# First mixture's gathers as float32r products for two quads of experts at once, and conditioning sums stored by chunk

## The chip, the cores and the metric

One core of a Trainium2 chip runs the kernel. The metric is the device time of one execution in microseconds (us). Its five engines run side by side: TensorE (PE; its loads of the stationary operand are listed apart as PEld), VectorE (DVE), ScalarE (ACT), GpSimd (POOL) and SyncE (SP), which here issues the loads of weights. 16 DMA engines move the data.

## The reference

Two transformer blocks for 256 tokens of width 1024, one after the other, in float32. Each has a conditioning vector, a token mixer (attention and a state-space branch in the first, two kinds of attention in the second) and a mixture of 32 experts. What the change touches, cut down:

```python
# conditioning, both blocks: one row times a 1024 x 6144 matrix
mod = silu(c) @ ada_w + ada_b            # six vectors of 1024: sh1, sc1, g1, sh2, sc2, g2

# mixture of the first block: each token goes to 2 of 32 experts of width 256
h   = rms_norm(x, norm2_g) * (1 + sc2) + sh2
xs  = h[tokens of expert e]              # gather
y_e = (silu(xs @ w_gate[e]) * (xs @ w_up[e])) @ w_down[e]
x   = x + g2 * sum over experts of weight * y_e, put back at the tokens
```

## The kernel before, in words

**Weights.** All large weights stream through a ring of buffers of 2 MB (128 partitions x 4096 floats). `Ring` keeps a list of pieces in the order of their use, and SyncE issues a piece's loads (line 132) as soon as a buffer is free; a buffer is free when `ring.done()` has let go of the oldest piece in use and the engines have finished reading it. During the first mixture the ring has five lasting buffers, `NR1 = 3` more in the pool `ringq` (these take no piece from "ka", the second block's first, on), and one in `ringt` that serves until the first context piece. `ringt` takes the place of the pool `pr`, in which the routing's small tiles lie, so it can be filled when the routing is done with them.

**First mixture.** The experts are worked on in 8 quads of four, with 32 places for each expert, so a quad has 128 rows. Where an expert has more than 32 tokens, the quad is run again for the rest (`extras`, in a branch taken when the register `nv` is positive; in this data for quads 0 and 7). The order of a quad q is:

- `gather1(q)` selects the tokens. `Sm`, 0 or the token's factor of normalisation, is compared out of the positions `posm1`; 16 products on TensorE (two halves of tokens n, eight slices c of the width) multiply it with `xv1[:, n, c, :]`, the tokens themselves. The stationary operand is the token slice, whose 128 elements stand 8 floats apart, since the slices are `x1.rearrange("t n (p c) -> t n c p", c=8)`. VectorE and ScalarE in turn copy the product to `xT`, with scale and shift. `Sw` is the selection times the routing weight, transposed on TensorE and copied to `sT` for the way back.
- `up1(q)` multiplies by gate and up weights (four pieces; a buffer is let go of after each), `act1` forms silu(gate) * up, `turn1` transposes it, `down1` multiplies by the down weights (two pieces, freed at the quad's end) and adds the result to `acc` at the tokens by `sT`.

The gather of quad q + 1 stands between `act1(q)` and `turn1(q)`, and fills TensorE while the activation is formed. In quad 0 the routing weights (`weights1`) and the count of extra blocks (`extra_blocks1`, which writes `nx1`, from which `nv` is read) are computed behind the first products, by `first1`. In quads 2, 3 and 4 products for the context tokens (`ctx0` to `ctx2`, with pieces of their own) stand ahead of the quad. The second mixture (`gather2`, lines 2510 to 2526) gathers two items at a time from two float32r parts of the normalised tokens, `xh` and `xl`; this step stays as it is.

**Conditioning.** A half vector of 512 is computed in one of two ways. `mod_rows` multiplies on TensorE into four rows of partial sums, which ScalarE copies to `rows`, and `pick` adds these up while it turns the result into a column layout. For the others ScalarE, VectorE and GpSimd scale and add the weights' slices (`vectors_on` in the first block, `conditions` in the second), GpSimd's last addition writes `sums` or `part`, and `mod_sum` adds over the partitions. `pick` (8 groups) and `mod_sum` (16 groups) are each eight products on TensorE of a slice `[:, c, :]` of 64 columns, as the stationary operand, with one or two moving columns. The 512 elements lie in the order (p c), so a slice's elements stand 8 floats apart.

**Order.** Up to the first gather, and from the second block on, PE, ACT and DVE run in the order in which the code is written; in between, within the first mixture, a scheduler may move instructions within a block of code, and each engine then runs its own list in order.

Of the kernel before, what the change touches and what calls it, by code (L numbers as in the profile page):

```python
# [22 lines left out]
D = 1024  # L23
T = 256
NEG = -1e30
NR1 = 3
NR3 = 2
NU = 3
MOD0 = 1
# [128 lines left out]
def _body(tc, nc, a, off, es, stop, dump):  # L158
# [11 lines left out]
    def trps():  # L170
        return ps("tr", 2)
# [273 lines left out]
    def used(key):  # L445

        released.add(key)
        while ring.used < ring.loaded and ring.pieces[ring.used][0] in released:
            ring.done()

    def mod_rows(key, lhs, into=None):

        w = ring.get(key).rearrange("p (c f) -> p c f", c=8)
        pt = mmps()
        for c in range(8):
            j = c % 4
            PE.matmul(pt[32 * j:32 * j + 32, :], bcast(lhs[:, c, :], [P, 32]), w[:, c, :], start=(c < 4), stop=(c >= 4), tile_position=(0, 32 * j))
        used(key)
        rows = into[:, :512] if into is not None else pp.tile([P, 512], F32, tag="modrows", bufs=2, name="rows")
        S.copy(rows, pt)  # L460
        return rows

    def pick(pt, h, rows, sel=None):

        sel = k("ecol") if sel is None else sel
        n = sel.shape[1]
        rv = rows.rearrange("q (p c) -> q c p", c=8)
        for c in range(8):
            PE.matmul(pt[64 * h:64 * h + 64, n * c:n * c + n], rv[:, c, :], sel, start=True, stop=True, tile_position=(0, 64 * h))

# [4 lines left out]
    def mod_sum(s, h, dst, bias):  # L475

        r = slice(64 * h, 64 * h + 64)
        pt = trps()
        sv = s.rearrange("q (p c) -> q c p", c=8)
        for c in range(8):  # L480
            PE.matmul(pt[r, c:c + 1], sv[:, c, :], k("ones")[:, 0:1], start=True, stop=True, tile_position=(0, 64 * h))
        add_bias(dst[r], pt[r], bias[r])
# [631 lines left out]
    def vectors_on():  # L1114

        pending = None
        for tag, v, h in vectors:
# [17 lines left out]
            for c in range(0, 8, 2):  # L1135
                S.activation(w[:, c], w[:, c], AF.Identity, scale=cs[:, c])
                if c:
                    G.tensor_tensor(w[:, 0], w[:, 0], w[:, c], op=ALU.add)
                    V.scalar_tensor_tensor(w[:, 1], w[:, c + 1], cs[:, c + 1], w[:, 1], op0=ALU.mult, op1=ALU.add)
                else:  # L1140
                    V.tensor_scalar(w[:, 1], w[:, 1], cs[:, 1], None, op0=ALU.mult)
                if c == 6:
                    G.tensor_tensor(sums, w[:, 0], w[:, 1], op=ALU.add)
                    used(key)
                if c == 4 and pending:
                    pending()
                    pending = None
                yield
# [452 lines left out]
    def all_tokens(xn, rstd, A, sh, n, hT):  # L1601
# [3 lines left out]
        for h in range(2):  # L1605
# [3 lines left out]
            for c in range(4):  # L1609
                cc = 4 * h + c  # L1610
                V.tensor_scalar(hT[:, cc], pt[:, P * c:P * c + P], A[:, cc:cc + 1], sh[:, cc:cc + 1], op0=ALU.mult, op1=ALU.add)

    def gather1(q, slots, tag, sT=None, between=None):

        Sm = pw1.tile([P, 2, 4, 32], F32, tag="Sm", name="Sm")
        Sw = pw1.tile([P, 2, 4, 32], F32, tag="Sw", name="Sw")
        e4 = slice(4 * q, 4 * q + 4)  # L1620
        for n in range(2):
            V.tensor_tensor(Sw[:, n], bcast(posm1[:, n, e4, None], [P, 4, 32]), bcast(slots[:, None, :], [P, 4, 32]), op=ALU.is_equal)
            V.tensor_scalar(Sm[:, n], Sw[:, n], rstd2[:, n:n + 1], None, op0=ALU.mult)  # L1623
            if between is None:
                V.tensor_tensor(Sw[:, n], Sw[:, n], bcast(W1[:, n, e4, None], [P, 4, 32]), op=ALU.mult)
        xT = pw1.tile([P, 8, P], F32, tag="xT" + tag, name="xT")
        for c2 in range(2):
            pt = mmps() if tag else ps("sc", 2)
            for cc in range(4):
# [15 lines left out]
        for n in range(2):  # L1645
            PE.transpose(pt[:, P * n:P * n + P], Sw[:, n].rearrange("p e s -> p (e s)"), ident)
        if sT is None:
            sT = pw1.tile([P, 2, P], F32, tag="sT", bufs=2, name="sT")
        S.copy(sT, pt[:, :T].rearrange("p (c s) -> p c s", c=2))
        return xT, sT  # L1650

# [9 lines left out]
        return pg  # L1661

    def act1(pg, tag):
        act = pw1.tile([P, 256], F32, tag="act" + tag, name="act")
# [35 lines left out]

    def first1(xT):
        pg.append(up1(0, xT, ""))
        weights1()
        extra_blocks1()

    nxt = gather1(0, iota[:, 0:32], "", between=first1)
    ordered.close()
    expand(gc[:, 1, :, 0], g2b)
    r1.close()
# [109 lines left out]
    for q in range(8):  # L1819
# [17 lines left out]
        xT, sT = nxt  # L1837
# [4 lines left out]
        def extras():  # L1842
            with tc.If(nv > 0):  # L1843
                turn1(act1(up1(q, gather1(q, iota[:, 32:64], "x", sTx)[0], "x"), "x"), aTx)


        if q > 0:
            extras()
        act = act1(up1(q, xT, "", True) if q else pg[0], "")
        if q == 0:  # L1850
            extras()
            ring.done(4)
        if q < 7:
            nxt = gather1(q + 1, iota[:, 0:32], "")
        aT = pw1.tile([P, 2, P], F32, tag="aT", name="aT")
        turn1(act, aT)
        if q < 7:
            down1(q, aT, sT, q == 0, "")
        with tc.If(nv > 0):
# [75 lines left out]
    def conditions():  # L1935

        ready, fresh = None, 0
        for i in range(9):
# [10 lines left out]
            for c in range(0, 8, 2):  # L1949
                if i < 8:  # L1950
# [4 lines left out]
                    else:  # L1955
                        V.tensor_scalar(w[:, 1], w[:, 1], cs2[:, 1, 0:1], None, op0=ALU.mult)
                    if c == 6:
                        G.tensor_tensor(s, w[:, 0], w[:, 1], op=ALU.add)
# [893 lines left out]
```

## Time and profile before

| | |
|---|---|
| median of 3 runs | 2046.55 us (2046.46 to 2049.3) |
| profiled execution | 2040.22 us |
| its span, first to last instruction | 2038.5 us |
| PE busy | 1767.2 us, 87% |
| DVE, ACT, POOL busy | 854.2, 544.2, 258.6 us |
| granted clock of PE, mean | 0.931 |

The span is divided among stages: start and first attention block (to 466 us), first mixture (466 to 766), second attention block (to about 1060), second mixture (to the end). A share of busy time is a mean over these, so each stage is read by itself. Matmuls are pipelined, and float32 products are recorded as two matmuls each.

### The profile page before, as it was taken

What the parts mean: (1) busy time and instruction counts of PE and PEld (TensorE: products, weight loads), DVE (VectorE), ACT (ScalarE), POOL (GpSimd) and SP (SyncE); (2) the same over time, 40 slices, a digit from 0 to 9 for tenths busy, and PEclk for the clock granted to TensorE, in tenths of its full rate; (3) what the DMA queues carried; (4) which work ended last, traced back from release to release, by engine and by line L of the source; (5) the groups of instructions that cost most, each with busy time, mean ns of one, the idle gap of its engine ahead of it and who ended that gap; (6) DMA issues with size and microseconds to landing.
All of it is one profiled execution on the core that took longest, in us unless ns stands there. A gap on an engine that the chain in (4) does not pass through costs nothing. (4 is left out here: it accounts for less than half of the span.)

```text
span 2038.5 us, 25531 instructions
## 1 busy us (share of the span) xinstructions
PE 1767.2 (87%) x10043; PEld 990.5 (49%) x10043; DVE 854.2 (42%) x1832; ACT 544.2 (27%) x1184; POOL 258.6 (13%) x232
## 2 busy tenths in 40 slices
PE   5898999998898997899999689886899889999865
PEld 3766777876445536678864123332233333333211
DVE  7998878543312237886644112211121221221112
ACT  4442566332001115565532011110021111121001
POOL 2576312110000003630110000000000000000000
PEclk8898889898999998899979899998899999999986
DMA  8634235867889977743347999999999999899996
GB/s 262 232 114 161 99 124 179 276 239 271 319 319 395 393 294 214 256 172 94 151 167 326 420 420 419 425 422 422 416 422 419 421 423 419 340 420 418 424 421 252
DMA packets 172666, 630.82 MB, mean 309 GB/s; under 512 B 25424, under 2 KB 32016, under 8 KB 152048
## 3 DMA queue, kind: packets, MB, share of 16 engines
q1 hardware_dynamic: 172112, 628.04, 79.3%
q8 instruction: 89, 1.46, 0.3%
q10 hardware_dynamic: 288, 0.52, 0.1%
q0 software_dynamic: 128, 0.39, 0.1%
q14 instruction: 49, 0.40, 0.1%
HBM read 627.88 MB, written 1.05 MB: 309 GB/s over the span
## 5 line engine op out<-in xcount | busy, mean ns | idle before, releaser
L2553 PE MATMUL mm<-w,xT 128*64 128x512 f32 x1472 | 329.3, 601 | 1.3 <-DMA w<-in_w_gu 1.3
L2553 PEld LDWEIGHTS mm<-w,xT 128*64 128x64 f32 x1472 | 102.8, 138 | 204.2 <-issue 197.4
L2644 PE MATMUL o<-w,aT 128*64 128x512 f32 x640 | 150.7, 606 | 2.5 <-DMA w<-in_w_dn 2.5
L2587 PE MATMUL mm<-w,xT 128*32 128x512 f32 x768 | 104.6, 675 | 39.9 <-DMA w<-in_w_gu 39.9
L2562 DVE TENSOR_SCALAR g<-mm 128x512 f32<-128x512 f32 x23 | 15.9, 692 | 262.7 <-PE mm L2553 262.7
L2821 POOL TENSOR_TENSOR fin<-acc,fin 128x512 f32<-128x512 f32 x1 | 1.3, 1275 | 975.6 <-DVE acc L2819 975.6
L718 DVE TENSOR_TENSOR lo<-w,hi 128x512 fp32r<-128x512 f32 x126 | 102.2, 824 | 26.9 <-ACT hi L717 24.9
L705 PE MATMUL mm<-hTh,scratch 128*128 128x256 f32 x392 | 98.3, 317 | 10.0 <-DVE scratch L718 10.0
L717 ACT CAST hi<-w 128x512 fp32r<-128x512 f32 x126 | 76.7, 620 | 62.0 <-PE mm L705 54.2
L2619 PE MATMUL o<-w,aT 128*32 128x512 f32 x384 | 69.1, 752 | 25.7 <-DMA w<-in_w_dn 23.9
L2644 PEld LDWEIGHTS o<-w,aT 128*64 128x64 f32 x640 | 45.1, 139 | 87.5 <-issue 80.3
L2564 ACT ACTIVATE s<-g 128x512 f32<-128x512 f32 x23 | 14.5, 632 | 272.9 <-DVE g L2562 272.9
L705 PEld LDWEIGHTS mm<-hTh,scratch 128*128 128x128 f32 x392 | 71.7, 204 | 28.1 <-issue 14.1
L1657 PE MATMUL mm<-w,xT 128*32 128x512 f32 x640 | 74.4, 612 | 6.6 <-DVEq L1843 2.7
L2659 DVE SCALAR_TENSOR_TENSOR yl<-yy,wc,yh 128x512 fp32r<-128x512 f32 (+1 forms) x30 | 21.4, 748 | 137.4 <-ACT yh L2658 137.2
L2587 PEld LDWEIGHTS mm<-w,xT 128*32 128x32 f32 x768 | 23.0, 117 | 108.1 <-DMA w<-in_w_gu 61.9
L705 PE MATMUL mm<-hT3h,lo 128*128 128x256 f32 x192 | 60.6, 316 | 8.7 <-DVE lo L718 6.1
L2649 ACT COPY yy<-o 64x512 f32<-64x512 f32 x40 | 23.2, 580 | 157.6 <-PE o L2644 157.2
L1632 PEld LDWEIGHTS sc<-Sm,x 128*128 128x128 f32 x256 | 61.6, 334 | 6.6 <-issue 5.0
L2674 DVE TENSOR_TENSOR acc<-acc,sc 128x512 f32<-128x512 f32 x56 | 37.0, 685 | 66.4 <-PE sc L2666 66.4
L1632 PE MATMUL sc<-Sm,x 128*128 128x128 f32 x256 | 63.1, 410 | 1.3 <-DVE Sm L1623 1.2
L705 PE MATMUL mm<-scratch 128*128 128x256 f32 x216 | 63.8, 295 | 0.0
(706 smaller groups left out, 3532.0 us busy)
## 6 DMA issues: line engine op xcount, KB each, us to landing
w<-in_w_gu SPq DMA_DIRECT2D x128, 2048.0 KB, 20.3
w<-in_w_dn SPq DMA_DIRECT2D x63, 2048.0 KB, 23.2
w<-in_w_in SPq DMA_DIRECT2D x20, 2048.0 KB, 9.5
w<-in_moe_w_gate SPq DMA_DIRECT2D x32, 1024.0 KB, 10.5
w<-in_moe_w_up SPq DMA_DIRECT2D x32, 1024.0 KB, 12.5
w<-in_moe_w_down SPq DMA_DIRECT2D x32, 1024.0 KB, 13.8
w<-in_ada_w SPq DMA_DIRECT2D x12, 2048.0 KB, 9.8
w<-in_w_mod SPq DMA_DIRECT2D x12, 2048.0 KB, 8.9
```

The lines of the kernel that those rows point to most:

```text
L705: PE.matmul(out, x, y, start=start and i == 0, stop=stop and i == 2)
L717: S.copy(hi, src)
L718: return parts, lambda: V.tensor_tensor(lo, src, hi.bitcast(F32), op=ALU.subtract)
L1632: PE.matmul(pt[:, P * cc:P * cc + P], xv1[:, n, c, :], Sm[:, n].rearrange("p e s -> p (e s)"), start=(n == 0), stop=(n == 1))
L1657: PE.matmul(pg[32 * j:32 * j + 32, :].rearrange("p (j f) -> p j f", j=2), xT[:, c, 32 * j:32 * j + 32], w[:, c % 2], start=(c == 0), stop= ...
L2553: PE.matmul(pg[i][64 * j:64 * j + 64, :], bcast(ident[:, q:q + 1], [P, 64]) if c < 0 else xT[:, c, :], bgu if c < 0 else w[:, o:o + 512], ...
L2587: PE.matmul(pg[32 * t:32 * t + 32, :], xT[:, c, :], w[:, 512 * ij:512 * ij + 512], start=False, stop=(c == 7), tile_position=(0, 32 * t))
L2619: PE.matmul(pd[32 * t:32 * t + 32, :], aT[:, f % 4, 2 * (1 - e) + f // 4, :], w[:, 512 * j:512 * j + 512], start=False, stop=(f == 7), til ...
L2644: PE.matmul(pd[64 * j:64 * j + 64, :], aT[:, f % 4, f // 4, :], w[:, 512 * j:512 * j + 512], start=False, stop=(f == 7), tile_position=(0, ...
L2649: S.copy(y[:, 512 * j:512 * j + 512], pd[64 * j:64 * j + 64, :])
L2659: V.scalar_tensor_tensor(yl[:, o], y[:, o], back[1], yh[:, o].bitcast(F32), op0=ALU.mult, op1=ALU.subtract)
L2674: V.tensor_tensor(o, o, pc, op=ALU.add)
```

## The change

- **Gathers.** `normalised1`, called in `first1` behind the first products and ahead of `weights1`, splits the normalised tokens into float32r parts `xh1` and `xl1`, each slice contiguous. `gather1s` then gathers two quads at once: a selection `Sms` of 256 columns of 0 and 1, 32 float32r products, four banks of PSUM, `xTs` of two quads. `back1s` forms `Sw` and `sT` of both. It is called in quads 0, 2, 4 and 6, for (1, 2), (3, 4), (5, 6) and (7, 7). In odd quads nothing stands between `act1` and `turn1`. `gather1` stays for quad 0 and for the extra tokens.
- **Buffers.** `NR1` goes from 3 to 2, so seven lasting buffers are left. Some tiles share tags (`Sw` and both activations have "act"), and in quad 0 `turn1` comes ahead of `extras`.
- **Conditioning.** `rows`, `sums` and `part` are written in the order (c p), so that the slices that `pick` and `mod_sum` load are contiguous; ScalarE's copy and GpSimd's last addition write with a spacing of 64 floats.

```diff
-NR1 = 3
+NR1 = 2
...
+    def by_chunk(t):
+
+        return t.rearrange("q (c p) -> q p c", c=8)
...
-        S.copy(rows, pt)
+        S.copy(by_chunk(rows), pt.rearrange("q (p c) -> q p c", c=8))
...
-        rv = rows.rearrange("q (p c) -> q c p", c=8)
+        rv = rows.rearrange("q (c p) -> q c p", c=8)
...
-        sv = s.rearrange("q (p c) -> q c p", c=8)
+        sv = s.rearrange("q (c p) -> q c p", c=8)
...
-                    G.tensor_tensor(sums, w[:, 0], w[:, 1], op=ALU.add)
+                    G.tensor_tensor(by_chunk(sums), w[:, 0].rearrange("q (p c) -> q p c", c=8), w[:, 1].rearrange("q (p c) -> q p c", c=8), op=ALU.add)
...
+    xh1 = pw1.tile([P, 2, 8, P], F32R, name="xh1")
+    xl1 = pw1.tile([P, 2, 8, P], F32R, name="xl1")
+
+    def normalised1():
+        for n in range(2):
+            S.activation(xh1[:, n], xv1[:, n], AF.Identity, scale=rstd2[:, n:n + 1])
+            V.scalar_tensor_tensor(xl1[:, n], xv1[:, n], rstd2[:, n:n + 1], xh1[:, n].bitcast(F32), op0=ALU.mult, op1=ALU.subtract)
+
+    def gather1s(qs):
...
+        xT = pw1.tile([P, 8, T], F32, tag="xT", name="xTs")
+        for c0 in range(0, 8, 2):
+            pt = ps("sc", 2)
+            for c in range(2):
+                for n in range(2):
+                    for x in (xl1, xh1):
+                        PE.matmul(pt[:, T * c:T * c + T], x[:, n, c0 + c, :], Sm[:, n], start=(n == 0 and x is xl1), stop=(n == 1 and x is xh1))
+            for c in (c0, c0 + 1):
+                i = pt[:, T * (c - c0):T * (c - c0) + T]
+                if c % 2:
+                    S.activation(xT[:, c], i, AF.Identity, scale=A2[:, c:c + 1], bias=sh2[:, c])
+                else:
+                    V.tensor_scalar(xT[:, c], i, A2[:, c:c + 1], sh2[:, c], op0=ALU.mult, op1=ALU.add)
+        return xT, lambda: back1s(qs, xT, Sm)
...
         pg.append(up1(0, xT, ""))
+        normalised1()
         weights1()
...
         act = act1(up1(q, xT, "", True) if q else pg[0], "")
+        aT = pw1.tile([P, 2, P], F32, tag="aT", name="aT")
         if q == 0:
+            turn1(act, aT)
             extras()
             ring.done(4)
-        if q < 7:
-            nxt = gather1(q + 1, iota[:, 0:32], "")
-        aT = pw1.tile([P, 2, P], F32, tag="aT", name="aT")
-        turn1(act, aT)
+        if q % 2 == 0:
+            _, backs1 = gather1s((q + 1, min(q + 2, 7)))
+        if q:
+            turn1(act, aT)
+        if q % 2 == 0:
+            quads = backs1()
```

How this stands on the engines, at three places. ScalarE (ACT) in quad 0, behind the copies of the first gather, before (`ge` and `gsc` are the routing weights, `g2b` an expanded gain, `act` the activation):

```order
L1637 ACTIVATE xT<-sc,sh_132,A_134 128x128 x4
L1566 ACTIVATE ge_4087,gsc_4088<-lg,gsc_4088 128x4
L1568 ACTIVATE gsc_4088<-gsc_4088 128x1
L1566 ACTIVATE ge_4118,gsc_4119<-lg,gsc_4119 128x4
L1568 ACTIVATE gsc_4119<-gsc_4119 128x1
L1665 ACT_TABLE_LOAD
L1665 ACTIVATE act<-mm 128x256
L1649 COPY sT<-tr 128x256
L491 COPY g2b<-mm 128x4x128 x2
```

and now:

```order
L1689 ACTIVATE xT<-sc,sh_132,A_134 128x128 x4
L1623 ACTIVATE xh_4170<-x_68,rstd_3796 128x1024 x2
L1570 ACTIVATE ge_4087,gsc_4088<-lg,gsc_4088 128x4
L1572 ACTIVATE gsc_4088<-gsc_4088 128x1
L1570 ACTIVATE ge_4118,gsc_4119<-lg,gsc_4119 128x4
L1572 ACTIVATE gsc_4119<-gsc_4119 128x1
L495 COPY g2b<-mm 128x4x128 x2
L1701 COPY sT<-tr 128x256
L1717 ACT_TABLE_LOAD
L1717 ACTIVATE act<-mm 128x256
L1726 COPY aT<-tr 128x256
```

The two passes over all tokens stand ahead of the routing weights, the activation has moved behind the copies of `g2b` and `sT`, and its transposes' copy `aT` now belongs to this place.

TensorE (PE) from the end of the first products of quad 2 to its down products, before:

```order
L1657 MATMUL mm<-w_4624,xT 32x512 x8
L1632 MATMUL sc<-Sm,x_68 128x128 x16
L1646 MATMUL tr<-C,Sw 128x128 x2
L1673 MATMUL tr<-C,act 128x128 x2
```

and now, in the same place (16 of the products `sc<-Sms` stand ahead of the transposes of `act`, 16 behind):

```order
L1709 MATMUL mm<-w_4672,xTs 32x512 x8
L1640 MATMUL sc<-Sms,xl_4171 128x256
L1640 MATMUL sc<-Sms,xh_4170 128x256
...
L1725 MATMUL tr<-C,act 128x128 x2
L1640 MATMUL sc<-Sms,xl_4171 128x256
...
L1659 MATMUL tr<-C,Sw 128x128
L1736 MATMUL mm<-w_4752,aT 32x512
L1659 MATMUL tr<-C,Sw 128x128 x2
```

One block of 16 became 32 shorter products with the transposes laid between them; in quad 1 the place between first products and transposes is empty.

SyncE (SP) from quad 1's first piece on, before:

```order
L132 DMA w_4158<-in_moe_w_gate 128x4x512
L132 DMA w_4158<-in_moe_w_up 128x4x512
L132 DMA w_4161<-in_moe_w_gate 128x4x512
L132 DMA w_4161<-in_moe_w_up 128x4x512
L132 DMA w_4287<-in_moe_w_gate 128x4x512
L132 DMA w_4287<-in_moe_w_up 128x4x512
L1840 TENSOR_LOAD nx_3800
```

and now:

```order
L132 DMA w_4158<-in_moe_w_gate 128x4x512
L132 DMA w_4158<-in_moe_w_up 128x4x512
L132 DMA w_4290<-in_moe_w_gate 128x4x512
L132 DMA w_4290<-in_moe_w_up 128x4x512
L1893 TENSOR_LOAD nx_3800
```

Ahead of the branch of quad 0 two pieces of quad 1 are issued where three were.

## Rows read from the trace of the kernel before

**Rows 1.** four stretches: busy us of PE, PEld, DVE, ACT, POOL; clock, DMA share, GB/s

```profile
205.00:440.00 235.00, 220.60 (x1526) 179.00 (x1525) 162.56 (x458) 120.16 (x294) 60.11 (x47) 0.91 0.54 177
466.00:766.00 300.00, 273.44 (x1562) 153.90 (x1562) 80.83 (x200) 41.14 (x100) 1.40 (x2) 0.98 0.88 331
570.00:745.00 175.00, 159.20 (x918) 88.09 (x914) 41.46 (x98) 21.24 (x52) 1.40 (x2) 0.98 1.02 386
795.00:925.00 130.00, 116.06 (x774) 95.65 (x773) 110.34 (x230) 74.07 (x172) 57.21 (x51) 0.91 0.68 227
```

**Rows 2.** timeline of PE, first mixture: start, length in us, instructions

```profile
466.27 7.95 PE L1632 MATMUL sc<-Sm,x 128*128 128x128 f32 x32 [1.20 <-DVE Sm L1623]
474.15 7.07 PE L1657 MATMUL mm<-w,xT 128*32 128x512 f32 x64
...
483.37 7.86 PE L1632 MATMUL mm<-Sm,x 128*128 128x128 f32 x32
...
574.75 7.88 PE L1632 MATMUL sc<-Sm,x 128*128 128x128 f32 x32
...
731.22 7.07 PE L1657 MATMUL mm<-w,xT 128*32 128x512 f32 x64
...
763.77 1.12 PE L1693 MATMUL sc<-y,sT 128*128 128x512 f32 x2 [0.20 <-DVE acc L1695]
```

**Rows 3.** waits of PE from 466 to 766: total us, times, longest

```profile
PE mm L1684 <- ACT aT L1674: 6.5, 8, 0.9
```

**Rows 4.** timeline of SP: two issues of weight pieces

```profile
479.95 0.37 SPq L132 DMA_DIRECT2D w<-in_moe_w_gate  x1
...
493.36 0.38 SPq L132 DMA_DIRECT2D w<-in_moe_w_gate  x1
```

**Rows 5.** lines by shape, PEld: busy us, mean ns of one load

```profile
L1632 PEld LDWEIGHTS sc<-Sm,x 128*128 128x128 f32 x256 | 61.6, 334 | 6.6 <-issue 5.0 <-DVE Sm L1623 1.6
...
L2518 PEld LDWEIGHTS sc<-Sm,xh 128*128 128x128 f32 x112 | 21.9, 195 | 0.9 <-issue 0.8
...
L481 PEld LDWEIGHTS tr<-C,sums 128*64 128x64 f32 x128 | 16.1, 215 | 0.7
```

**Rows 6.** timeline of PE at three other places

```profile
217.29 2.08 PE L481 MATMUL tr<-C,sums 128*64 128x1 f32 x16
...
455.42 1.87 PE L1467 MATMUL mm<-rw,xr 128*128 128x36 f32 x16
...
1215.74 0.28 PE L2518 MATMUL sc<-Sm,xh 128*128 128x256 f32 x1
...
1217.41 0.28 PE L2518 MATMUL sc<-Sm,xh 128*128 128x256 f32 x1
```

**Rows 7.** lines by shape, ACT and then DVE, whole span

```profile
L2464 ACT ACTIVATE xT<-sc,sh,A 128x256 f32<-128x256 f32 x28 | 15.8, 563 | 22.1 <-DVE xT L2466 21.9
...
L2454 ACT ACTIVATE xh<-x,r 128x1024 fp32r<-128x1024 f32 x2 | 4.2, 2166 | 0.0
...
L460 ACT COPY rows<-mm 128x512 f32<-128x512 f32 x4 | 2.3, 580 | 7.1 <-PE mm L457 7.1
...
L491 ACT COPY fgb<-mm 128x512 f32<-128x512 f32 x2 | 2.2, 1080 | 8.0 <-PE mm L490 8.0
...
L2466 DVE TENSOR_SCALAR xT<-sc,A,sh 128x256 f32<-128x256 f32 x28 | 15.1, 541 | 13.5 <-PE sc L2518 13.5
...
L2455 DVE SCALAR_TENSOR_TENSOR xl<-x,r,xh 128x1024 fp32r<-128x1024 f32 x2 | 4.2, 2088 | 0.3 <-ACT xh L2454 0.3
```

**Rows 8.** timeline of DVE in the first quad

```profile
475.53 0.14 DVE L1565 TENSOR_SCALAR gsc<-t 128x1 f32<-128x1 f32 x1
...
479.64 0.16 DVE L1582 CAST nx<-qm 1x8 int32<-1x8 f32 x1
...
480.10 0.47 DVE L1643 TENSOR_TENSOR Sw<-Sw,W 128x128 f32<-128x128 f32 x2
```

**Rows 9.** waits of PE from 205 to 440 us

```profile
PE tr L1308 <- DVE e L1302: 4.2, 6, 1.5
```

More of the change, by code (lines that the diff above doesn't have):

```diff
@@ new lines, in gather1s @@
+    def gather1s(qs):
+        Sm = pw1.tile([P, 2, T], F32R, tag="Sms", name="Sms")
+        for i in range(2):
+            e4 = slice(4 * qs[i], 4 * qs[i] + 4)
+            for n in range(2):
+                V.tensor_tensor(Sm[:, n, P * i:P * i + P].rearrange("p (e s) -> p e s", e=4), bcast(posm1[:, n, e4, None], [P, 4, 32]),
+                                bcast(iota[:, None, 0:32], [P, 4, 32]), op=ALU.is_equal)
+        xT = pw1.tile([P, 8, T], F32, tag="xT", name="xTs")
+        for c0 in range(0, 8, 2):
+            pt = ps("sc", 2)
+            for c in range(2):
+                for n in range(2):
+                    for x in (xl1, xh1):
[7 more added lines that the diff above has]
+        return xT, lambda: back1s(qs, xT, Sm)
@@ new lines, in back1s @@
+    def back1s(qs, xT, Sm):
+        out = []
+        for i in range(1 if qs[0] == qs[1] else 2):
+            e4 = slice(4 * qs[i], 4 * qs[i] + 4)
+            Sw = pw1.tile([P, 2, 4, 32], F32, tag="act", name="Sw")
+            for n in range(2):
+                V.tensor_tensor(Sw[:, n], Sm[:, n, P * i:P * i + P].bitcast(F32).rearrange("p (e s) -> p e s", e=4),
+                                bcast(W1[:, n, e4, None], [P, 4, 32]), op=ALU.mult)
+            pt = trps()
+            for n in range(2):
+                PE.transpose(pt[:, P * n:P * n + P], Sw[:, n].rearrange("p e s -> p (e s)"), ident)
+            sT = pw1.tile([P, 2, P], F32, tag="sT", bufs=3, name="sT")
+            S.copy(sT, pt[:, :T].rearrange("p (c s) -> p c s", c=2))
+            out.append((xT[:, :, P * i:P * i + P], sT))
+        return out
@@ L1613, in gather1 @@
     def gather1(q, slots, tag, sT=None, between=None):
-        Sm = pw1.tile([P, 2, 4, 32], F32, tag="Sm", name="Sm")
-        Sw = pw1.tile([P, 2, 4, 32], F32, tag="Sw", name="Sw")
+        Sm = pw1.tile([P, 2, 4, 32], F32, tag="Sms", name="Sm")
+        Sw = pw1.tile([P, 2, 4, 32], F32, tag="act", name="Sw")
         e4 = slice(4 * q, 4 * q + 4)
@@ L1625, in gather1 @@
                 V.tensor_tensor(Sw[:, n], Sw[:, n], bcast(W1[:, n, e4, None], [P, 4, 32]), op=ALU.mult)
-        xT = pw1.tile([P, 8, P], F32, tag="xT" + tag, name="xT")
+        xT = pw1.tile([P, 8, T if not tag else P], F32, tag="xT" + tag, name="xT")[:, :, :P]
         for c2 in range(2):
@@ L1647, in gather1 @@
         if sT is None:
[L1648 removed]
+            sT = pw1.tile([P, 2, P], F32, tag="sT", bufs=3, name="sT")
         S.copy(sT, pt[:, :T].rearrange("p (c s) -> p c s", c=2))
@@ L1663, in act1 @@
     def act1(pg, tag):
-        act = pw1.tile([P, 256], F32, tag="act" + tag, name="act")
+        act = pw1.tile([P, 256], F32, tag="act", name="act")
         S.activation(act, pg[:, :256], AF.Silu)
@@ L1702, in first1 @@
         pg.append(up1(0, xT, ""))
+        normalised1()
         weights1()
         extra_blocks1()
-    nxt = gather1(0, iota[:, 0:32], "", between=first1)
+    quads = [gather1(0, iota[:, 0:32], "", between=first1)]
     ordered.close()
@@ L1836, in _body @@
             expand(fgc, fgb)
-        xT, sT = nxt
+        xT, sT = quads.pop(0)
         aTx = pw1.tile([P, 2, P], F32, tag="aTx", name="aTx")
@@ L1957, in conditions @@
                     if c == 6:
-                        G.tensor_tensor(s, w[:, 0], w[:, 1], op=ALU.add)
+                        G.tensor_tensor(by_chunk(s), w[:, 0].rearrange("q (p c) -> q p c", c=8), w[:, 1].rearrange("q (p c) -> q p c", c=8), op=ALU.add)
                         used(key)
```

## Prediction

> **What bounds the kernel now.** I first read the kernel by stretches [rows 1]: for each, the busy time of TensorE against the stretch, and the share of the DMA engines. Three stretches touch the change. From 205 to 440 us (first attention block, with twelve of the conditioning sums) TensorE is busy 220.6 of 235 us and the DMA share is 0.54: TensorE bounds it. From 795 to 925 us (second attention block, eight sums) TensorE has 116.1 of 130 us, VectorE 110.3, so the two are close. From 466 to 766 us, the first mixture, TensorE has 273.4 of 300 us, and the DMA share is 0.88. In its middle, 570 to 745 us, the DMA engines are full (1.02, 386 GB/s) while TensorE is still 91% busy. Next the waits: the longest in total of TensorE in the mixture is 6.5 us, for a copy of ScalarE, and no load of weights is in that list [rows 3]. So the mixture is bound by TensorE today, but the loads run at their full rate just behind it. That second limit decides what a shorter TensorE can bring.
>
> The sum is made in the profiled execution (2040.22 us, span 2038.5); the median of the runs shown is 2046.55, 6.33 us above it, and I carry the difference over unchanged. A change of 0.2%, 4.1 us, is about what this kernel's measurement can tell from none.
>
> **Gathers on TensorE.** A quad's gather is now 16 float32 products, recorded as 32 matmuls, and takes 7.95, 7.86 or 7.88 us in one piece [rows 2]. Seven of them (quads 1 to 7) go: 7 x 7.88 = 55.2 us. The quad 0 gather and the two for extra tokens (quads 0 and 7) stay. Four gathers of a pair of quads come, 32 float32r matmuls of 256 columns each. The second mixture already does this very step: 15 of its matmuls start from 1215.74 to 1217.41 us [rows 6], 0.119 us apart, so 32 take 3.8 us. A bank's two copies out of PSUM follow one another, 563 ns on ScalarE and 541 ns on VectorE [rows 7]; with two banks the third and fourth wait for them, and I take 5 us a pair, 20 us in all. (Bounds: 3.8, or 7 if the copies hold up each bank.) In quads 1, 3 and 5 no gather hides the activation between the first products and their transposes any more: about 1 us each, 3 us. TensorE alone is therefore 55 - 20 - 3 = 32 us shorter from quad 1 on.
>
> **First quad.** The split into two parts now stands, in program order, ahead of the routing weights. Its price is known from the same pair of instructions in the second mixture: 2166 ns on ScalarE and 2088 ns on VectorE for each half [rows 7], VectorE one half behind. Beginning when the copies of the first gather end, near 476 us, it is over at 476.1 + 2 x 2.17 + 2.09 = 482.6. The routing chain on VectorE, which began at 475.53, starts 7.1 us later; its count of extra blocks moves from 479.64 to 486.7 and the weighted selection, now done at 480.57, to 487.7 [rows 8]. TensorE was free for the extra gather at 483.37 [rows 2]. Now it waits for the transposes of that selection until 487.7, and behind them for the transposes of the first activation, which the change puts ahead of the extra tokens and which on ScalarE now queues behind the copy of the selection: some 4 us more of short instructions (estimate). The extra gather begins near 492.2: 9 us lost. Below nothing is excluded, since nothing hides it; above, 12, if the clock falls in the pause. TensorE's sum for the mixture is then 32 - 9 = 23 us shorter.
>
> **Loads.** One ring buffer goes, so during the first quad one piece of 2.1 MB fewer is fetched. The piece that SyncE issued at 479.95 moves with the count of extra blocks; the next, issued at 493.36 when the extra products let go of the first buffer [rows 4], moves to 502.4. From there 42.5 pieces are left (two of quad 1's gate and up weights, its two of down weights, six each for quads 2 to 7, and two and a half of context weights), 89.1 MB. At 386 GB/s that is 231 us, and I add 3 us for a gap when the ring is empty after the first quad: the last piece lands at 736, the last of gate and up weights two pieces (11 us) before it, at 725. What follows it today is the rest of the last quad, from the end of the extra products at 731.22 + 7.07 = 738.3 to 763.77 + 1.12 = 764.9 [rows 2], 26.6 us, plus 1.8 us for the last quarter of those products: 753. The same count for today's kernel, 41.5 pieces from 493.36, gives 736 against the 764.9 measured, so today the loads have 29 us in hand and afterwards nothing. TensorE's own limit is 764.9 - 23 = 742. The later one decides, 753, and since neither runs without hiccups I take 757: **8 us gained** of the 23. Bounds: 23, if loads never bind, and a loss of 18 (rival below).
>
> **Conditioning sums.** The 24 groups of `pick` and `mod_sum` each load eight slices of 64 columns, whose elements stand 32 bytes apart, and take 2.08 us for 16 records, 130 ns each [rows 6]. Spread columns load slowly here: 334 ns for 128 of them in the old gather against 195 ns for 128 contiguous ones in the second mixture's, and 215 ns for the 64 of the sums [rows 5]. A contiguous float32 operand with few moving columns is the router: 16 records in 1.87 us [rows 6], 117 ns for 128 columns, so 58 ns for 64. A group falls from 2.08 to 0.93 us: 1.15 us. Of TensorE's clock the rows show 0.91 of full in both stretches, before and behind the groups, and I leave that.
>
> How much counts? Twenty groups lie in the two stretches where TensorE is the busiest. Its waits there are short ones on VectorE (4.2 us over six for the softmax rows [rows 9]), one within 10 us or so of nearly every group. A wait swallows the gain if VectorE is itself the limit there, and passes it on if VectorE was waiting for TensorE; with VectorE at 69% of the first stretch and 85% of the second I take 0.55: 20 x 1.15 x 0.55 = 12.7. The four groups at the start wait for loads, and only the last counts: 1.15 less 0.5 for ScalarE's copy, which now writes spread elements (1080 against 580 ns [rows 7]). **13 us gained**; bounds 0 and 24. The sixteen sums of GpSimd also write spread elements, for which no row has a price; were every GpSimd instruction of the second stretch half as long again, it would be busy 86 of 130 us, and the sum is read only a vector later, so I take nothing.
>
> The Trainium skill, page "TensorE: Matmul & The Clock Gate", section "LDWEIGHTS (loading the stationary operand)", says that a load takes its number of columns divided by 1.2 in ns, and names no dependence on their spacing: 53 ns for 64. By that rule this part would gain nothing, and the sum would be 8 us; the 334 against 195 ns above speak against it.
>
> **Sum.** 8 + 13 = 21 us: 2040.22 - 21 = 2019 in the profiled execution, and 2046.55 - 21 = **2025.5 us** as the median of runs. What follows the mixtures' ends is shifted whole: the second mixture starts when its routing is known.
>
> **Rivals.** *Loads do not bind.* If seven buffers and 386 GB/s suffice, the mixture gains TensorE's 23 us, and with 13 the kernel takes 2010.5. For it: no wait on a load today [rows 3]. Against: full DMA engines in 175 of its 300 us [rows 1]. Chance 0.15.
>
> *The layout brings nothing*, because the waits behind each group swallow it or because spacing does not matter to a load of 64 columns: 8 us alone, 2038.5. For it: VectorE at 85% in the second stretch; against, the two load rows. Chance 0.15.
>
> *The missing buffer starves the queue* (slower). During the context products and the extra tokens, which use one buffer or none, TensorE frees little. If with one buffer less all pieces ahead land before the next is freed, the DMA engines idle for up to one more piece, 5.4 us, each time: some five times, 27 us, turning 8 gained into 18 lost, so 2051.5 with the sums' 13. It decides once these gaps pass 21 us together. For it: the share over the mixture, 0.88, shows such gaps already; against, most of them lie before 570 us. Chance 0.08.
>
> **Numbers.** My forecast has 0.62, its own range 2016 to 2035 (mixture from 0 to 15 us, sums from 7 to 18, not both at one end). Over all cases I give 2008 to 2042, which leaves out the slower rival and little else. Faster by over 0.2%: 0.85 (nearly all of the forecast, the first rival, most of the second); within: 0.06; slower: 0.09.
>
> **What would show it.** Right: new matmuls of the pair about 0.12 us apart; TensorE idle near 9 us between 483 and 492 us; waits of TensorE for gate, up and down weights in quads 5 and 6 (some 15 to 20 us), DMA full from about 505 to 735 us; the mixture 8 us shorter from its first gather to its last product, which then stands near 750 us as the sums shift it too; groups of the sums near 0.9 us. Wrong: no wait for a load, or groups still at 2 us, or DMA gaps of several us in every quad.

## The result, and the profile after

The changed kernel takes 2023.74 us (median of 4 runs, 2019.08 to 2027.47) against 2046.51 for the kernel before: ratio 0.9886, 95% interval 0.9862 to 0.9911, so 23 us or 1.1% faster. The prediction was 2025.5 us. The profiled execution took 2022.03 us with a span of 2020.0.

First the same stretches as in [rows 1], in the view by windows of the kernel after; the second line is the first mixture from its first gather to its last product, and the fourth a part of it. The columns are the stretch and its length, the busy us of PE, PEld, DVE, ACT and POOL, the granted clock, the DMA share and GB/s.

```profile
205.00:440.00 235.00, 216.07 (x1527) 173.36 (x1526) 171.61 (x469) 124.57 (x302) 59.69 (x48) 0.93 0.58 193
449.74:742.90 293.16, 250.70 (x1466) 119.27 (x1466) 78.30 (x175) 41.72 (x88) 1.40 (x2) 0.93 0.91 342
570.00:745.00 175.00, 146.29 (x824) 62.22 (x822) 43.02 (x88) 21.13 (x51) 1.40 (x2) 0.93 1.03 392
640.00:690.00 50.00, 36.60 (x200) 12.29 (x201) 7.60 (x17) 2.55 (x6) 0.00 (x0) 0.80 1.03 399
795.00:925.00 130.00, 113.43 (x807) 88.53 (x807) 110.71 (x248) 77.03 (x184) 45.48 (x45) 0.91 0.57 191
```

Two things are to be seen. The first gather starts at 449.74 us instead of 466.27 [rows 2]: 16.5 us are won before the mixture begins. The mixture lasts 293.16 us instead of 764.89 - 466.27 = 298.62 [rows 2]: 5.5 us are won in it. TensorE is busy 250.7 us there, so it is idle for 42.5; the DMA engines are full in its second half as before, and TensorE is no longer: 146.29 of 175 us against 159.20 [rows 1].

The timeline of TensorE in the first quad of the kernel after (start, length, and in brackets the idle time ahead with what ended it), to be read beside [rows 2, 8]:

```profile
449.74 7.95 PE L1684 MATMUL sc<-Sm,x 128*128 128x128 f32 x32 [1.20 <-DVE Sm L1675]
457.62 7.07 PE L1709 MATMUL mm<-w,xT 128*32 128x512 f32 x64
464.63 2.05 PE L494 MATMUL mm<-C,gc 128*128 128x128 f32 x16
470.54 0.66 PE L1698 MATMUL tr<-C,Sw 128*128 128x128 f32 x2 [3.86 <-DVE Sw L1695]
473.81 0.70 PE L1725 MATMUL tr<-C,act 128*128 128x128 f32 x2 [2.61 <-DVE act L1718]
475.39 7.91 PE L1684 MATMUL mm<-Sm,x 128*128 128x128 f32 x32 [0.88 <-DVE Sm L1675]
...
493.12 0.28 PE L1640 MATMUL sc<-Sms,xh 128*128 128x256 f32 x1
493.23 0.27 PE L1640 MATMUL sc<-Sms,xl 128*128 128x256 f32 x1
```

The extra gather (475.39) starts 25.65 us after the first gather; before it was 483.37 - 466.27 = 17.10 [rows 2]. The 8.6 us between are the pause that the prediction put at 9. Three waits for VectorE make up 7.35 us of it: 3.86 for the weighted selection, which comes behind the split; 2.61 for the activation, which on ScalarE now queues behind the copy of that selection; and 0.88 for the next selection. The last two lines are the new pair gather: one matmul each 0.12 us.

The waits of TensorE in the mixture of the kernel after (total us, times, longest), beside [rows 3]:

```profile
PE mm L1709 <- DMA w<-in_moe_w_up: 8.6, 3, 4.0
PE tr L1725 <- DVE act L1718: 8.3, 7, 2.6
PE tr L1698 <- DVE Sw L1695: 3.9, 1, 3.9
...
PE mm L1736 <- ACT aT L1726: 2.1, 4, 0.5
PE mm L1736 <- DMA w<-in_moe_w_down: 1.6, 2, 1.0
```

Loads stand in this list now, for 8.6 + 1.6 = 10.2 us; before there were none. They fall in quads 5 and 6, as the timeline of the same kernel shows:

```profile
639.94 5.36 PE L1709 MATMUL mm<-w,xTs 128*32 128x512 f32 x48 [1.21 <-ACTq L1896]
649.30 3.40 PE L1709 MATMUL mm<-w,xTs 128*32 128x512 f32 x16 [4.00 <-DMA w<-in_moe_w_up]
...
656.69 1.92 PE L1736 MATMUL mm<-w,aT 128*32 128x512 f32 x4 [0.98 <-DMA w<-in_moe_w_down]
...
676.18 2.98 PE L1709 MATMUL mm<-w,xTs 128*32 128x512 f32 x16 [2.21 <-DMA w<-in_moe_w_up]
681.56 3.64 PE L1709 MATMUL mm<-w,xTs 128*32 128x512 f32 x16 [2.40 <-DMA w<-in_moe_w_up]
```

In this stretch (640 to 690 us, above) the granted clock is 0.80: between its waits TensorE runs a part of the time at the lower of its two levels. The 48 products ahead of the longest wait take 5.36 us, 16 behind it 3.40.

The prediction's path ran through the last piece of gate and up weights. Its issue by SyncE, the same issue in the view of the DMA queue (KB, us to landing), and the extra products of quad 7, which use it first:

```profile
698.53 2.58 SPq L132 DMA_DIRECT2D w<-in_moe_w_up  x1
...
w<-in_moe_w_up SPq DMA_DIRECT2D x1, 1024.0 KB, 14.5
...
709.17 7.07 PE L1709 MATMUL mm<-w,xT 128*32 128x512 f32 x64
```

It lands at 713.0 us, about 1 us before the last quarter of these products needs it; the last product of the mixture ends 29.9 us later.

Last the conditioning sums: a group in the timeline of TensorE in the kernel after, beside the 2.08 us of [rows 6]:

```profile
214.94 1.09 PE L485 MATMUL tr<-C,sums 128*64 128x1 f32 x16
```

And lines by shape of the same kernel, of PEld, ACT and POOL in turn (busy us, mean ns of one), beside [rows 5, 7]:

```profile
L485 PEld LDWEIGHTS tr<-C,sums 128*64 128x64 f32 x128 | 8.3, 138 | 0.8
...
L464 ACT COPY sums<-mm 128x512 f32<-128x512 f32 x4 | 4.3, 1074 | 11.4 <-PE mm L461 11.4
...
L2015 POOL TENSOR_TENSOR part<-w 128x512 f32<-128x512 f32 x8 | 11.3, 1418 | 4.5 <-DVE w L2011 4.0
```

A load of 64 columns takes 138 ns instead of 215, a group 1.09 us instead of 2.08. ScalarE's copy pays for the spread writes as forecast (1074 against 580 ns); GpSimd's spread write costs nothing that shows (1418 ns; the kernel before has 1409 at that place).

### The profile page after: what moved, and what is told of

Read it like the earlier page. It is cut to its first block, busy times and chain, and to the rows that moved or that the text cites. A ratio compares the mean times of both kernels' runs of the same rounds, so it can differ in the third digit from the quotient of the medians.

```text
span 2020.0 us, 25309 instructions
## 1 busy us (share of the span) xinstructions
PE 1729.8 (86%) x9947; PEld 935.7 (46%) x9947; DVE 858.8 (43%) x1810; ACT 549.1 (27%) x1174; POOL 257.8 (13%) x232
## 5 line engine op out<-in xcount | busy, mean ns | idle before, releaser
L2610 PE MATMUL mm<-w,xT 128*64 128x512 f32 x1472 | 334.0, 608 | 0.0
L2644 PE MATMUL mm<-w,xT 128*32 128x512 f32 x768 | 105.2, 679 | 38.0 <-DMA w<-in_w_gu 38.0
L2878 POOL TENSOR_TENSOR fin<-acc,fin 128x512 f32<-128x512 f32 x1 | 1.3, 1272 | 980.7 <-DVE acc L2876 980.7
L1709 PE MATMUL mm<-w,xTs 128*32 128x512 f32 x448 | 56.7, 651 | 16.1 <-DMA w<-in_moe_w_up 8.6
L709 PE MATMUL mm<-hT3l,hi 128*128 128x256 f32 x192 | 56.1, 292 | 0.4 <-DVE hT3l L705 0.4
L709 PE MATMUL mm<-hT3h,hi 128*128 128x256 f32 x192 | 55.8, 291 | 0.0
## 6 DMA issues: line engine op xcount, KB each, us to landing
w<-in_moe_w_gate SPq DMA_DIRECT2D x32, 1024.0 KB, 14.1
```

Source lines behind the costliest of these rows:

```text
L709: PE.matmul(out, x, y, start=start and i == 0, stop=stop and i == 2)
L1709: PE.matmul(pg[32 * j:32 * j + 32, :].rearrange("p (j f) -> p j f", j=2), xT[:, c, 32 * j:32 * j + 32], w[:, c % 2], start=(c == 0), stop= ...
L2610: PE.matmul(pg[i][64 * j:64 * j + 64, :], bcast(ident[:, q:q + 1], [P, 64]) if c < 0 else xT[:, c, :], bgu if c < 0 else w[:, o:o + 512], ...
L2644: PE.matmul(pg[32 * t:32 * t + 32, :], xT[:, c, :], w[:, 512 * ij:512 * ij + 512], start=False, stop=(c == 7), tile_position=(0, 32 * t))
```

## The experiments

Two theories stood against each other. The prediction's: the gathers give TensorE more than 20 us, the loads take most of it back, and the sums give about 13 us. The other, from the two profiles alone: the sums give 16 to 18 us and the gathers 5. In the table the stretch of the mixture is from the start of the first gather to the end of the last product, in the profiled execution.

| kernel | median, us | ratio to before (95%) | mixture, us |
|---|---|---|---|
| after, first comparison | 2023.74 | 0.9886 (0.9862 to 0.9911) | 293.16 |
| after_again | 2020.64 | 0.9885 (0.9861 to 0.9910) | 292.09 |
| e1_gathers_alone | 2035.56 | 0.9947 (0.9931 to 0.9962) | 293.24 |
| e9_gathers_again | 2034.89 | 0.9962 (0.9946 to 0.9979) | 291.88 |
| e2_sums_alone | 2031.54 | 0.9928 (0.9913 to 0.9944) | 298.73 |
| e8_second_block | 2040.80 | 0.9977 (0.9964 to 0.9991) | 300.32 |
| e4_before_seven | 2044.86 | 0.9990 (0.9975 to 1.0005) | 301.88 |
| e3_split_early | 2020.46 | 0.9870 (0.9849 to 0.9891) | 287.35 |
| e3_again | 2017.17 | 0.9867 (0.9843 to 0.9891) | 286.82 |
| e7_long_runs | 2017.92 | 0.9879 (0.9854 to 0.9903) | 288.04 |

Two more, e5 and e6, have one run each, and their profiles alone are used.

**The gathers alone.** In the changed kernel, the sums go back to spread columns:

```diff
-        S.copy(by_chunk(rows), pt.rearrange("q (p c) -> q p c", c=8))
+        S.copy(rows, pt)
-        rv = rows.rearrange("q (c p) -> q c p", c=8)
+        rv = rows.rearrange("q (p c) -> q c p", c=8)
-        sv = s.rearrange("q (c p) -> q c p", c=8)
+        sv = s.rearrange("q (p c) -> q c p", c=8)
```

(and the two sums of GpSimd likewise).

> The changed kernel with the conditioning sums as they were (spread columns); gathers in pairs, seven ring buffers kept. By the prediction's own terms the mixture's part is 8 us: ratio to before 0.996. By the trace after, which has the mixture 5.5 us shorter (293.2 against 298.6 us from its first gather to its last product), 0.997. If instead the gathers carry nearly all of the gain and the sums little (the rival in which the layout brings nothing), 0.989 to 0.991. The sum groups should take about 2.08 us again.

> The gathers alone once more (sums with spread columns), because the first comparison gave 10.8 us (7.8 to 14.1) while the profiles put the mixture only 6 to 7 us shorter. By the profiles and by the prediction's 8 us the ratio is 0.996 to 0.997; by the first comparison 0.9947. If it comes out near 0.9947 again, some 4 us are gained outside the mixture.

Measured: 10.8 us (7.8 to 14.1) the first time and 7.8 us (4.3 to 11) the second. The prediction's 8 lies in both intervals; the mixture in the two profiles is 5.4 and 6.7 us shorter than 298.62. So the first figure stands at the upper end, and at least half of the gain is seen in the mixture; whether a few microseconds more come from elsewhere is below what these runs can tell.

**The sums alone.** The opposite edit, on the kernel before.

> The kernel before with the conditioning sums kept contiguous, gathers and eight buffers as they were. By the prediction 13 us of gain, ratio 0.9936, of which about 8 before the first mixture and 5 in the second attention block. By the trace after, 16.5 us before the first mixture and 1.6 in the second block: 0.991 to 0.992. If the layout brings nothing, 0.998 to 1.002. Groups of 1.09 us instead of 2.08.

Measured: 14.7 us (11.5 to 17.8), and the mixture is as it was (298.73). With the gathers' 8 to 11 this is the whole change: the parts add up. The 16.5 us that the two profiles show ahead of the mixture were too many, and the runs show why: from the first sum group to the first gather the six profiled kernels with spread sums in the first block took 242.4 to 249.0 us (mean 246.1), and the kernel before happened to be the longest of them. The seven with contiguous sums took 233.4 to 240.4 (mean 236.2). So 9.9 us arrive at the mixture.

TensorE's busy time in this stretch falls by more, from 227.6 to 212.0 us in the mean, and its idle time rises from 18.5 to 24.2. The twelve groups save 12 x 0.99 = 11.9 of these 15.6 us; other instructions became shorter too. Clearest are the 64 products of `mod_rows`, by lines of the kernel before and of the kernel after, from the first sum group to the first gather:

```profile
L457 PE MATMUL mm<-w,cs 128*32 128x512 f32 x64 | 10.7, 801 | 0.0
...
L461 PE MATMUL mm<-w,cs 128*32 128x512 f32 x64 | 7.7, 598 | 0.0
```

They take 739 to 802 ns in the six kernels with spread sums and 598 ns in all seven others. The first 16 stand right behind a sum group, in the timelines of before and after:

```profile
377.95 3.50 PE L457 MATMUL mm<-w,cs 128*32 128x512 f32 x16
...
368.91 1.92 PE L461 MATMUL mm<-w,cs 128*32 128x512 f32 x16
```

And by windows, over the stretch that holds all 64 and the four groups of `pick` there, before and after:

```profile
377.00:420.50 43.50, 43.50 (x311) 34.15 (x311) 14.30 (x28) 11.99 (x19) 4.96 (x4) 0.87 0.94 299
...
368.80:403.50 34.70, 34.03 (x312) 27.27 (x311) 15.51 (x29) 14.18 (x20) 5.09 (x5) 1.00 1.03 329
```

The granted clock is 1.00 instead of 0.87, though the profile shows TensorE without a pause there before (43.50 us busy of 43.50). In all runs these products go with the layout; what lowers the clock beside spread sums was not tried by itself.

**The eight sums of the second block alone.** On the kernel before:

```diff
-                        G.tensor_tensor(s, w[:, 0], w[:, 1], op=ALU.add)
+                        G.tensor_tensor(s.rearrange("q (c p) -> q p c", c=8), w[:, 0].rearrange("q (p c) -> q p c", c=8), w[:, 1].rearrange("q (p c) -> q p c", c=8), op=ALU.add)
```

with `mod_sum` reading contiguous columns for these eight only.

> The kernel before with only the eight sums of the second attention block kept contiguous. By the prediction's share of 0.55 they give 5 us: ratio 0.9975. By the profiles so far, in which the stretch from the mixture's end to the eighth group is 151 to 153.3 us with contiguous sums and 151.7 to 155.1 with spread ones, 1 to 2 us: 0.999 to 0.9995. If they give all that a group saves, 8 us, 0.996, and then the first block's twelve gave only some 6 of the 14 us that the sums alone gave.

Measured: 4.7 us (1.8 to 7.4), where the prediction's share gave 5. The profiles show less: from the mixture's end to the end of the eighth group the mean is 153.1 us over eight kernels with contiguous sums in this block, and 155.5 over five with spread ones, 2.4 us, with single runs from 152 to 157. From the mixture's end to the end of the span the means are 1276.8 and 1277.2, with single runs from 1272 to 1281. So the 2.4 us lie inside the interval of the timing, and whether more is gained behind the eighth group no profile shows.

**One buffer less, nothing else.** On the kernel before:

```diff
-NR1 = 3
+NR1 = 2
```

> The kernel before with seven ring buffers instead of eight, nothing else. By the prediction today's loads have 29 us in hand, so a buffer less costs little: ratio 1.000 to 1.002, with few or no waits of TensorE for weights. By the rival in which the missing buffer starves the queue, up to 27 us: ratio 1.005 to 1.013, with gaps of several us in the DMA engines after each freed buffer.

Measured: 0.9990 (0.9975 to 1.0005), no cost that can be told. Its mixture is 3.3 us longer than in the kernel before (301.88), but TensorE waits for no load in it; e8, with the mixture untouched, has 300.32, so part of this is scatter. The loads of the kernel before had time in hand, as the prediction counted, though perhaps not its 29 us: e8, whose mixture is that of the kernel before, has one wait of 1.7 us for a load. The rival of the starving queue falls as it was put, with today's loads; what the missing buffer costs in the changed kernel, where the loads bind, was not run. A piece fetched earlier would there be worth at most its own 5.4 us (estimate: 2.1 MB at the 392 GB/s of 570 to 745 us).

**Fewer loads.** Of each quad's two pieces of down weights only one is loaded, in the kernel before (e5) and in the changed kernel (e6):

```diff
-        for e in (4 * q, 4 * q + 2):
+        for e in (4 * q,):
             pieces.append((("dn1", e), lambda t, e=e: load_dn1(t, e)))
...
-                    w = ring.get(("dn1", 4 * q + j // 2 * 2))...
+                    w = ring.get(("dn1", 4 * q))...
...
-        ring.done(2)
+        ring.done()
```

(These kernels leave out half of the down weights; half of the experts multiply by another's.)

> The kernel before with half of the first mixture's down weights left out: the second pair of experts of each quad computes with the first pair's weights, 8 of 51 pieces of 2.1 MB fewer. In the kernel before, TensorE waits for no load in the mixture, so by the theory that TensorE alone bounds it the mixture stays at 298.6 us (within 1). If loads bound it too, it gets up to 43 us shorter (8 pieces of 5.4 us).

> The changed kernel with the same half of the down weights left out. By the prediction's step TensorE's own limit is 23 us under the kernel before, so the mixture falls from 293.2 to 275.6 us, with the first quad's stall of 8.6 us still in it, and TensorE's 10.2 us of waits for up and down weights go. If loads do not bind and the gain was lost elsewhere, it stays at 291 to 294 us. If besides the waits the lower clock behind them costs time, the products at 636 to 651 ns each fall back to the 595 to 612 ns that they took before.

The view by windows over the mixture, of e5:

```profile
464.42:762.58 298.16, 272.91 (x1562) 154.66 (x1562) 79.53 (x197) 40.12 (x98) 1.41 (x2) 0.97 0.76 281
```

And of e6:

```profile
457.15:726.76 269.61, 238.52 (x1466) 116.15 (x1466) 78.31 (x175) 41.77 (x88) 1.41 (x2) 0.96 0.86 316
```

With fewer loads the kernel before stays where it was (298.16 against 298.62), and the changed kernel falls from 293.16 to 269.61 us. So the loads do not bind the mixture before, and they take at least 23 us of it after. This is the clearest of the runs: it shows TensorE's own gain (298.2 - 269.6 = 28.6 us) and what the loads take back, apart. Both are lower bounds, since in e6 too TensorE waits 3.2 us for loads:

```profile
PE mm L1709 <- DMA w<-in_moe_w_down: 2.2, 2, 1.2
...
PE tr L1725 <- DMA w<-in_moe_w_up: 1.0, 1, 1.0
```

The view by lines of the kernel after, for the products of TensorE in the mixture (busy us, mean ns of one, idle time before them):

```profile
L1709 PE MATMUL mm<-w,xTs 128*32 128x512 f32 x448 | 56.7, 651 | 16.1 <-DMA w<-in_moe_w_up 8.6 <-DVEq L1896 2.7 <-ACTq L1896 2.6
L1736 PE MATMUL mm<-w,aT 128*32 128x512 f32 x256 | 39.1, 636 | 3.6 <-ACT aT L1726 2.1 <-DMA w<-in_moe_w_down 1.6
```

And the same of e6:

```profile
L1709 PE MATMUL mm<-w,xTs 128*32 128x512 f32 x448 | 51.9, 610 | 7.2 <-DVEq L1896 2.7 <-DMA w<-in_moe_w_down 2.2 <-ACTq L1896 1.4
L1736 PE MATMUL mm<-w,aT 128*32 128x512 f32 x256 | 32.4, 596 | 2.1 <-ACT aT L1726 2.1
```

Of the 23.6 us between the two, idle time is 42.5 - 31.1 = 11.4 and busy time 250.7 - 238.5 = 12.2, nearly all of it in these two groups (4.8 + 6.7): the same instructions take longer. The granted clock over the mixture is 0.93 in the one and 0.96 in the other. So the loads cost their waits and about as much again in slower products; that these are slower because of the clock behind the waits is read from the rows, not tried by itself, and how much of it would have been waits at the full clock stays open.

**The split earlier.** In the changed kernel, the split is issued behind the selection of the first gather and ahead of its copies, where ScalarE is idle from 442 to 454 us and VectorE from 450 to 454:

```diff
+        if ahead is not None:
+            ahead()
         xT = pw1.tile([P, 8, T if not tag else P], F32, tag="xT" + tag, name="xT")[:, :, :P]
...
     def first1(xT):
         pg.append(up1(0, xT, ""))
-        normalised1()
         weights1()
...
-    quads = [gather1(0, iota[:, 0:32], "", between=first1)]
+    quads = [gather1(0, iota[:, 0:32], "", between=first1, ahead=normalised1)]
```

> The changed kernel with the split of the tokens placed ahead of the first gather, where ScalarE and VectorE have nothing to do (12 us and 4 us idle), instead of ahead of the routing weights. The extra gather should then start about 17 us after the first gather, not 25.6. If the last load sets the end of the mixture and its issues hang on the extra products of the first quad (the prediction's step), the mixture is 8 us shorter than after's 293.2: ratio 0.984 to 0.985. If the stall is only traded for later waits on loads, the mixture stays within 2 us and the ratio at 0.988. If the loads do not bind at all, again 8 us, but without TensorE's waits for weights growing.

> The changed kernel once more, beside the next run on the same chip. By the sum of the two parts run alone (0.9947 and 0.9928), 0.9875; by the first comparison 0.9886. Sum groups 1.09 us; from the first gather to the last product 293 us.

> The changed kernel with the split ahead of the first gather, once more, beside the changed kernel itself. By its first profile its mixture is 5.8 us shorter than the changed kernel's (287.35 against 293.16), which would be 0.9971 of the changed kernel: 0.984 to 0.986 of before. If what it gains there is given back in the load-bound second mixture, within 0.001 of the changed kernel.

The timeline of VectorE in the first of the two runs of this version:

```profile
451.13 4.06 DVE L1624 SCALAR_TENSOR_TENSOR xl<-x,rstd,xh 128x1024 fp32r<-128x1024 f32 x2
455.11 0.40 DVE L1693 TENSOR_SCALAR xT<-sc,A,sh 128x128 f32<-128x128 f32 x1
```

And that of TensorE:

```profile
450.75 7.96 PE L1686 MATMUL sc<-Sm,x 128*128 128x128 f32 x32 [1.20 <-DVE Sm L1675]
...
468.70 0.50 PE L1727 MATMUL tr<-C,act 128*128 128x128 f32 x2 [0.83 <-DVE act L1720]
470.08 7.86 PE L1686 MATMUL mm<-Sm,x 128*128 128x128 f32 x32 [0.88 <-ACT g2b L495]
```

The split now ends as the first copies are due. The extra gather starts 19.3 us after the first instead of 25.65, and the mixture lasts 287.35 and 286.82 us, 4.7 to 6.3 less than in the two profiles of the changed kernel: of 6.3 us of pause taken away, most arrives, though the DMA engines are full behind it. That is the prediction's step, that the issues of loads hang on the extra products of the first quad. SyncE's next issue, in the changed kernel and in this version, moved from 35.7 to 29.3 us after the first gather:

```profile
485.43 0.38 SPq L132 DMA_DIRECT2D w<-in_moe_w_gate  x1
...
480.06 0.38 SPq L132 DMA_DIRECT2D w<-in_moe_w_gate  x1
```

By time the version is 0.9870 and 0.9867 of the kernel before, both times some 3 us under the changed kernel's median (2023.74 and 2020.46; 2020.64 and 2017.17), but the intervals overlap: the mixture is shown to be shorter, the kernel only likely to be faster.

**Longer packets.** On the version with the early split, each piece of gate and up weights holds two experts and four column chunks instead of four experts and two:

```diff
-        r = t.rearrange("p (j e f) -> p j e f", j=2, e=4)
-        return [(r[:, j], moe1[j][4 * q:4 * q + 4].rearrange("e (p c) f -> p e (c f)", p=P)[:, :, 512 * k:512 * k + 512]) for j in range(2)]
+        h, e0 = k // 2, 4 * q + k % 2 * 2
+        r = t.rearrange("p (j e f) -> p j e f", j=2, e=2)
+        return [(r[:, j], moe1[j][e0:e0 + 2].rearrange("e (p c) f -> p e (c f)", p=P)[:, :, 1024 * h:1024 * h + 1024]) for j in range(2)]
...
-            if release and c % 2:
-                ring.done()
+            if release and c % 4 == 3:
+                ring.done(2)
```

> The version with the early split, and each piece of gate and up weights cut the other way: two experts and four column chunks instead of four experts and two, so that a DMA packet is 4 KB and not 2 KB; the matmuls are the same, but the first four need two pieces, and buffers come free two at a time. In the trace a 2 KB packet takes 87 ns and the second mixture's 4 KB packet 164 ns, 6% less per byte, or 0.33 us a piece. If the loads bind the whole mixture, some 27 pieces make it 9 us shorter than the early split's 287: 278 to 281 us, ratio 0.982 to 0.983. If TensorE sets the time behind the loads, 287 us and 0.987. If the coarser release costs more than the faster packets give, 289 us or more and a ratio above 0.988.

The view by windows of the early split, 570 to 700 and 450 to 550 us:

```profile
570.00:700.00 130.00, 105.11 (x581) 45.19 (x580) 28.95 (x64) 13.29 (x29) 1.40 (x2) 0.92 1.04 395
...
450.00:550.00 100.00, 89.49 (x554) 49.59 (x558) 31.16 (x80) 14.47 (x33) 0.00 (x0) 0.97 0.73 272
```

And of this version:

```profile
570.00:700.00 130.00, 107.22 (x595) 48.63 (x588) 29.78 (x62) 13.30 (x29) 1.41 (x2) 0.96 1.02 405
...
450.00:550.00 100.00, 85.91 (x509) 51.14 (x510) 35.25 (x105) 18.28 (x35) 0.56 (x1) 0.93 0.70 259
```

Nothing was gained: the mixture lasts 288.04 us. The full stretch does move more, 405 against 395 GB/s, though by 2.5% and not by the 6% of a packet; the start moves less, 259 against 272 (this execution reached the mixture 7 us later, which is part of that). The coarser release was changed together with the packets, so the run does not say which of the two held the other back.

## Why the prediction was right, step by step

**Gathers on TensorE.** The pair gathers ran 0.12 us apart, as read from the second mixture [rows 6], and TensorE's busy time fell by 272.91 - 238.52 = 34.4 us where loads are out of the way (e5 against e6); the prediction had 55.2 - 20 = 35.2. The microsecond lost in each of quads 1, 3 and 5 was a mistake: the transposes do wait longer for VectorE (8.3 us in all, 2.6 of them in the first quad, against 2.9 before), but the wait for ScalarE's `aT` behind them falls from 6.5 us [rows 3] to 2.1. Idle time grew by 31.1 - 25.3 = 5.8 us, not by the 3 + 9 of the prediction, so TensorE's sum is at least 28.6 us and not 23 (3.2 us of this idle time are the waits for loads that e6 still has).

**First quad.** Right in place and size: 8.6 us against 9, and the next load issue 485.43 - 449.74 = 35.7 us after the first gather against 493.36 - 466.27 = 27.1 [rows 2, 4].

**Loads.** The limit is the loads, as e6 shows, and the path to it was counted nearly right. The last of the gate and up weights was to land 725 - 466.3 = 258.7 us after the first gather [rows 2], with 28.4 us of work behind it: 287 us, or 291 with the 4 us for hiccups. It landed after 263.3 us, 29.9 us were left, and the mixture took 293.16. So it became 5.5 us shorter (5.4 to 6.7 in the four profiles of the changed kernel and of the gathers alone) where 8 was said. The end keeps to this landing: in after_again, e1, e9, e3 and e3_again it comes 28.8 to 29.8 us behind it, while the landing itself lies anywhere from 257.0 to 264.4 us; in the kernel before it came 37.7 us behind. What TensorE waited for is not this piece, though, but those of quads 5 and 6: the last wait for a load ends at 681.6 us, and in quad 7 the gather of the extra tokens (7.9 us) gives the loads time, so that the last piece comes 1 us early. The waits were put at 15 to 20 us and are 10.2; as much again lies in slower products at the lower clock, for which the prediction had no term in the later quads. TensorE's own limit was wrong too (28.6 us or more gained, not 23). Neither changes the end, because the later limit decides. The DMA share from 505 to 735 us was 1.01, as forecast.

**Conditioning sums.** The mechanism was right and its size nearly so: 1.09 us a group against 0.93, thus 0.99 us saved for 1.15, and a larger share of it counted, (14.7 - 0.6) / (20 x 0.99) = 0.71 for 0.55 (0.6 us for the groups at the start, as forecast). The two misses pull opposite ways, so it is in part luck that 13 came so near. In the first block 9.9 of 11.9 us arrive. Waits did swallow some of it, as forecast: idle time rose by 5.7 us, and waits for VectorE's `e` from 4.2 us [rows 9] to 9.4. But other instructions became 3.7 us shorter, 2.8 of it in the products of `mod_rows`, beside which the clock rose from 0.87 to 1.00; the prediction had seen a lower clock in its rows and left it at nothing. The rule of the Trainium skill, page "TensorE: Matmul & The Clock Gate", section "LDWEIGHTS (loading the stationary operand)", would have given this part nothing; the sums alone gave 14.7 us, and the load fell from 215 to 138 ns with the spacing, so the measurement decides against it.

**Sum and rivals.** 8 + 13 was forecast; alone the parts gave 8 to 11 and 14.7, together 23. That the loads do not bind falls with e6, that the layout brings nothing with e2, and that the missing buffer starves the queue and makes the kernel slower with e4 and with the result itself. What follows the mixture was to be shifted whole: from its end to the end of the span the kernels took 1272 to 1281 us, the kernel before 1273.6 and the kernel after 1277.1 and 1272.3. No loss shows there, but within that scatter neither would a few microseconds, nor does the gain of the eight sums.

## What to carry to other kernels

Where an engine is the bound and the transfers run at their full rate just behind it, work out both limits before and after: here 28.6 us taken from TensorE became 5 to 7, and a run with fewer loads showed the rest at once. Work that prepares a faster step belongs in a hole of the engines that do it: the same split cost 8.6 us ahead of the routing weights and 2 us a few instructions earlier. Two profiles cannot share out a gain of 1%, since a stretch without any edit differed by 6 us between executions; change one part at a time and time it.

## What the runs showed of the hardware

Waits for weights came with slower products: with 10.2 us of waits in the mixture the same up and down products took 651 and 636 ns each, and 610 and 596 ns with 3.2 us of waits; the granted clock was 0.80 from 640 to 690 us, where the waits are, against 0.98 from 570 to 745 us before [rows 1]. A load of 64 float32 columns takes 138 ns when they are contiguous and 215 ns when they stand 32 bytes apart. Beside such spread groups the granted clock was 0.87 though the profile shows TensorE busy throughout (377 to 420.5 us before), and 1.00 beside contiguous ones (368.8 to 403.5 us after); 16 products right behind a group took 3.50 and 1.92 us. A copy of ScalarE that writes 128x512 elements 256 bytes apart takes 1074 ns instead of 580, and a sum of GpSimd that writes so 1418 ns, against 1409 with contiguous writes.
